# One recurrent and one convolutional projection in plain fp32 instead of a three-part split, and the convolution's taps divided anew

## The chip, the cores and the metric

The kernel runs on one core of a Trainium2 chip. Its time is device microseconds from launch to end; the time shown is the median of three runs. In the texts PE is TensorE (matrix products into PSUM), DVE is VectorE, ACT is ScalarE, POOL is GpSimd and SP is the engine whose queue issues the loads.

## The reference

A two-layer encoder works on 272 tokens (256 and 16 learned ones in front) of 1024 channels. Each layer is a token mixer and a channel mixer, each followed by `h = layer_norm(alpha * h + f(h))`. What matters here, cut down:

```
# layer 0: recurrent mixer
gate, u = split(h @ w_in)                  # w_in: 1024 x 2048
u = depthwise_conv(u, 4 taps)
r, i = sigmoid(u @ w_a), sigmoid(u @ w_x)  # eight blocks of 128, two directions
a = exp(-8 r softplus(-lam));  b = sqrt(1 - a^2) * i * u
h = scan forward + scan backward           # h_t = a_t h_(t-1) + b_t
mix = (h * gelu(gate)) @ w_out
# layer 1: convolution mixer
h = glu(x @ w_pw1 + b)                     # w_pw1: 1024 x 2048
h = depthwise_conv(h, 31 taps)
mix = silu(layer_norm(h)) @ w_pw2 + b
# both layers: expert mixer (256 wide products over u and v, the bulk of the time)
```

The output is the 256 later tokens, in fp32.

## The kernel before

Activations lie with the channels on the partitions: a tensor is eight blocks (NB) of 128 channels by 272 tokens. A projection of 1024 by 1024 is eight output blocks; the weights of each, 128 x 1024 fp32 (512 KB), come by one DMA into one of four buffers named `raw`.

Most products are made by `linears`. `load_split` makes of each weight block a rounded part `hi` in fp32r (on ACT, or on DVE where hi_on says "v") and on DVE or POOL the remainder `lo`; the activations are split the same way into `xs(k, 0)` and `xs(k, 1)`. For an output block, PE then adds up three times eight matmuls: hi by hi, hi by lo, lo by hi. With `defer=2` the first two blocks are interleaved so that the parts that are ready early go first. The buffer `raw` is free again once both parts are made.

*Recurrent mixer* (`recurrent`). x comes by four DMAs and is split block by block by `split_x`. The first eight blocks of w_in give u; `gates` takes each from PSUM (a ring of three banks), makes the four-tap convolution on DVE (L365, L369), two products per direction in plain fp32 (L376 into `pr`, L378 into `pi`, four banks), four activations on ACT, three fused operations on DVE and one on POOL. `roots` takes the square roots for four blocks at once, `scans` runs the two scans on DVE, `gelu` takes the second eight blocks of w_in (each in a bank of its own), and `gated` multiplies and splits the result into hh and hl for the output projection w_out. That goes through `linears` with `late=True`, so that its first two blocks leave the products of the last channel block to the end. `shift_in` adds the result to the residual and keeps the sums for the layer norm, whose mean is a product with a matrix of ones (L279).

*Convolution mixer* (`conformer`). `normed` centres and scales, and `norm_split` makes of it hi and lo parts (L316, L318, L324) and the fp32 value in place (L323). `conv_glu` projects through `linears` (the gating half before the other half of each block, a ring of five banks); `consume` makes the sigmoid on ACT (L1037) and the gate product hp on DVE (L1043). The 31 taps of a block are then made in one of two ways. On DVE: fused multiply-adds of 256 columns (L1071) into two sums that are added at the end (L1072). On PE: one product per tap with a diagonal matrix that ACT makes (`diagonal`, L1006). PE_TAPS says how many taps of each block PE takes; for the blocks in SPLIT the diagonals and hp are split, three fp32r products a tap, for the others it is one fp32 product. `add_up` (L763) forms the sum over blocks for the mean (L288).

What sets the order: each engine runs its instructions in a fixed order that a planner lays down before the run. It takes the instructions in program order as priority and starts each where its costs say that operands and buffers are there; `issue_after` forces an instruction behind another. An engine whose next instruction has to wait makes everything behind it wait.

Of the kernel before, what the change touches and what calls it, by code (L numbers as in the profile page):

```python
# [7 lines left out]
F32 = mybir.dt.float32  # L8
# [3 lines left out]
AF = mybir.ActivationFunctionType  # L12
OP = mybir.AluOpType
# [4 lines left out]
P = 128  # L18
D = 1024
NB = D // P  # L20
# [18 lines left out]
FULL = (("v", 1024),)  # L39
SQ_AT = 4  # L40
PE_TAPS = (0, 0, 0, 0, 12, 31, 31, 31)
SPLIT = (6, 7)
CONV_ORDER = (5, 4, 6, 7)
NEG = -3.0e38
# [15 lines left out]
class Trunk:  # L60
# [105 lines left out]
    def linears(self, srcs, xs, n, lo_on, consume, defer=0, hi_on="a", ring=(0, 1, 2), first=None, late=False):  # L166
# [7 lines left out]
        for idx, src in enumerate(srcs):  # L174
# [22 lines left out]
            else:  # L197
# [3 lines left out]
                consume(idx, ps[:, :n])  # L201

    def split_x(self, src, hi, lo, hi_on="a"):
        nc = self.nc
        if hi_on == "a":
            nc.scalar.activation(hi, src, AF.Copy)  # L206
        else:
            nc.vector.tensor_copy(hi, src)
        nc.vector.tensor_tensor(lo, src, hi.bitcast(F32), op=OP.subtract)  # L209
# [118 lines left out]
    def recurrent(self):  # L328
        tc, nc, a = self.tc, self.nc, self.a
        n = T0  # L330
        with tc.tile_pool(name="mix0", bufs=2) as sp:
            x = sp.tile([P, NB, n], F32, name="x0", bufs=1)
            xs = self.new_xs()
            self.early.append(self.load(a["w_in"][0]))
# [4 lines left out]
            self.early.append(self.load(a["w_in"][2]))  # L339
            for k in range(NB):  # L340
                self.split_x(x[:, k, :], xs(k, 0), xs(k, 1), hi_on="av"[k % 2])
            gw = sp.tile([P, 4, NB, P], F32, name="gw", bufs=1)
# [8 lines left out]
            o = _OFF["lru_b_a"]  # L351
# [69 lines left out]
            def gelu(b, ps):  # L421
# [5 lines left out]
                if b >= 4:  # L427
# [3 lines left out]
                    if b == NB - 1:  # L431
                        self.pins = [None, g.ins]
                    raw.clear()

            self.linears([a["w_in"][b] for b in range(NB)], xs, n, FULL, gates, hi_on="aaavvvvv")
            self.linears([a["w_in"][NB + b] for b in range(NB)], xs, n, FULL, gelu,
                         ring=(7, 0, 1, 2, 3, 4, 5, 6))
            for b in range(NB):
# [529 lines left out]
    def conformer(self, acc):  # L968
        tc, nc, a = self.tc, self.nc, self.a
        n, m = T0, SEQ  # L970
        with tc.tile_pool(name="mix1", bufs=2) as sp:
            x = sp.tile([P, NB, n], F32, name="x1", bufs=1)
            self.collect(sp, acc, x, n)
            self.left_pool.__exit__(None, None, None)
            xs = self.new_xs()
            self.norm_split(sp, x, n, lambda k: self.col("ln_ffn_g", k), lambda k: self.col("ln_ffn_b", k),
                            lambda k: xs(k, 0), lambda k: xs(k, 1), shifted=True)
            y = sp.tile([P, NB, m], F32, name="cy", bufs=1)
            self.conv_glu(sp, xs, y)
            x2 = x[:, :, META:]  # L980
# [43 lines left out]

    def conv_glu(self, sp, xs, y):
        tc, nc, a = self.tc, self.nc, self.a
# [6 lines left out]
        def consume(i, ps):  # L1033
# [6 lines left out]
            else:  # L1040
# [5 lines left out]
                if b in SPLIT:  # L1046
                    parts[b] = [sp.tile([P, n + HALO], F32R, tag=f"hs{i}", name=f"hs{i}", bufs=len(SPLIT)) for i in range(2)]
                    self.split_x(hp, *parts[b])

        self.linears([a["pw1"][b + o] for b in range(NB) for o in (NB, 0)], xs, n, FULL, consume, defer=2,  # L1050
                     ring=(0, 1, 2, 7, 6))
        s = META - HALO
# [4 lines left out]
        for b in range(NB):  # L1057
            taps = range(KCONV - len(on_pe[b]))
            if not taps:
                continue  # L1060
            z1 = y[:, b, :]
            z2 = sp.tile([P, m], F32, tag="odd", name="odd", bufs=2)
            for k in taps:
                z = z2 if k % 2 else z1
                w, h = self.col("conf_dw_w", k * NB + b), hps[b][:, s + k:s + k + m]
                if k == 0:
                    nc.vector.tensor_scalar(z, h, w, self.col("conf_dw_b", b), op0=OP.mult, op1=OP.add)
                elif k < taps[0] + 2:
                    nc.vector.tensor_scalar(z, h, w, None, op0=OP.mult)
                else:  # L1070
                    nc.vector.scalar_tensor_tensor(z, h, w, z, op0=OP.mult, op1=OP.add)  # L1071
            nc.vector.tensor_tensor(z1, z1, z2, op=OP.add)  # L1072
            if not on_pe[b]:
                self.add_up(sp, y, b, m)
# [116 lines left out]
```

## Time and profile before

| | us |
|---|---|
| median of three runs | 1856.66 (1856.33 to 1856.78) |
| the profiled execution | 1857.75 |
| its span, first to last instruction | 1856.0 |
| PE busy | 1793.9 (97%) |
| DVE busy | 1562.6 (84%) |
| ACT busy | 940.7 (51%) |
| POOL busy | 484.6 (26%) |

The busy time of PE counts matmuls from start to end, and neighbours overlap; the rate is read from one start to the next. The recurrent mixer fills the first 128 us, the convolution mixer lies at 905 to 1070 us; the rest is the two expert mixers.

### The profile page before, as it was taken

The numbers are of one execution on the slowest core, as the hardware profiler recorded it, in microseconds if no ns is written. First come the engines' busy times: TensorE is split into PE (matmuls) and PEld (weight loads), VectorE is DVE, ScalarE is ACT, GpSimd is POOL, SyncE is SP. The second block draws the span as 40 slices with busy tenths as digits, with TensorE's granted clock in tenths as the row PEclk, the third lists the DMA queues.
The fourth block names the chain that finished last, engine by engine and source line by source line (L and its number), as shares of the span: only waits on it lengthen the run. The fifth ranks groups of instructions, "written<-read, shape, count | busy, mean of one in ns | idle before, by whom it ended". The sixth has DMA issues, their size and how long they took to land.

```text
span 1856.0 us, 35898 instructions
## 1 busy us (share of the span) xinstructions
PE 1793.9 (97%) x13929; PEld 1714.4 (92%) x13929; DVE 1562.6 (84%) x2849; ACT 940.7 (51%) x1537; POOL 484.6 (26%) x330
## 2 busy tenths in 40 slices
PE   7899999999999999999999999999999999999997
PEld 6789998999999999999889899999999999999996
DVE  8985997889998787777699869998889987878776
ACT  5744544554444444885471545444554444445442
POOL 1112899100001232321000017993000012433310
PEclk9999999999999999999999999999999999999999
DMA  5345466855557888987541354668555568989883
GB/s 195 112 150 171 160 195 194 282 171 166 168 169 239 304 315 274 318 285 272 184 136 35 106 179 155 188 204 273 184 168 171 171 226 302 324 303 342 300 278 127
DMA packets 110235, 394.15 MB, mean 212 GB/s; under 512 B 12144, under 2 KB 13296, under 8 KB 109936
## 3 DMA queue, kind: packets, MB, share of 16 engines
q1 hardware_dynamic: 91632, 324.74, 53.6%
q0 software_dynamic: 18432, 67.12, 10.1%
q8 instruction: 109, 1.79, 0.4%
q14 instruction: 62, 0.51, 0.1%
HBM read 386.50 MB, written 5.31 MB: 211 GB/s over the span
## 4 chain that ended last, share of the span: by engine, by line
PE 81%; DVE 7%; issue 6%; POOL 3%; DMA 2%; ACT 1%; POOLq 0%; SPq 0%; DVEq 0%; ACTq 0%
PE u L172 42%; PE acc L632 20%; PE acc L636 11%; POOL lo L144 2%; PE cv L1081 2%; DVE lo L144 2%; DMA raw<-peer_v 2%; PE g L590 1%; PE g L591 1%; PE sps L522 1%; PE wide_ps L865 1%; DVE rows L900 0%; PE acc L671 0%; POOL rows L891 0%; ACT t L385 0%
## 5 line engine op out<-in xcount | busy, mean ns | idle before, releaser
L137 ACT ACTIVATE hi<-raw 128x1024 fp32r<-128x1024 f32 x587 | 620.4, 1059 | 641.1 <-PE u L172 236.2
L144 DVE TENSOR_TENSOR lo<-raw,hi 128x1024 fp32r<-128x1024 f32 x500 | 612.4, 1229 | 172.4 <-PE acc L636 63.2
L172 PE MATMUL u<-xs,hi 128*128 128x224 f32 (+3 forms) x5120 | 656.0, 279 | 15.6 <-ACT xs L206 6.4
L172 PEld LDWEIGHTS u<-xs,hi 128*128 128x128 f32 x5120 | 617.5, 191 | 20.5 <-ACT xs L318 7.2
L632 PE MATMUL acc<-w,hi 128*128 128x480 f32 (+1 forms) x1984 | 458.5, 373 | 2.0 <-DVE w L209 2.0
L632 PEld LDWEIGHTS acc<-w,hi 128*128 128x128 f32 x1984 | 354.5, 188 | 35.3 <-DVE w L209 2.3
L172 PE MATMUL u<-xs,lo 128*128 128x240 f32 (+3 forms) x2560 | 355.7, 279 | 13.6 <-POOL lo L144 10.7
L172 PEld LDWEIGHTS u<-xs,lo 128*128 128x128 f32 x2560 | 322.5, 191 | 17.5 <-POOL lo L144 12.8
L636 PEld LDWEIGHTS acc<-w,lo 128*128 128x128 f32 x2048 | 267.8, 190 | 16.9 <-DVE lo L144 6.0
L636 PE MATMUL acc<-w,lo 128*128 128x240 f32 (+1 forms) x2048 | 272.1, 274 | 3.7 <-DVE lo L144 3.6
L144 POOL TENSOR_TENSOR lo<-raw,hi 128x1024 fp32r<-128x1024 f32 x92 | 241.5, 2640 | 84.0 <-ACT hi L137 66.8
L891 POOL DMA_INDIRECT rows<-u_rows,ids x64 | 94.5, 1476 | 638.4 <-DVE sv L782 450.0
L891 POOL DMA_INDIRECT rows<-peer_v,ids x64 | 104.9, 1638 | 226.1 <-DVE few_out L926 118.6
L597 ACT ACTIVATE act_b<-g 128x368 f32<-128x368 f32 (+43 forms) x58 | 22.6, 390 | 113.4 <-DVE act_b L560 95.2
L900 DVE SCALAR_TENSOR_TENSOR rows<-rows,wide 128x1024 f32<-128x1024 f32 x64 | 78.9, 1233 | 0.6 <-DMA rows<-u_rows,ids 0.6
L926 DVE SCALAR_TENSOR_TENSOR few_out<-rows,act,few_out 128x1024 f32<-128x1024 f32 x60 | 76.7, 1278 | 0.8 <-DMA rows<-peer_v,ids 0.8
L573 DVE TENSOR_TENSOR AB<-iota,iT 128x2048 f16<-128x2048 f16 x58 | 70.4, 1217 | 0.1
L316 POOL TENSOR_SCALAR xs<-x,par 128x272 fp32r<-128x272 f32 (+1 forms) x6 | 6.0, 998 | 228.3 <-DVE x L308 165.7
L590 PE MATMUL g<-AB 128*128 128x128 f16 x464 | 58.6, 220 | 0.0
L591 PE MATMUL g<-Bl,AB 128*128 128x128 f16 x464 | 58.0, 219 | 0.0
L209 DVE TENSOR_TENSOR w<-act_b,w 128x960 fp32r<-128x960 f32 (+1 forms) x32 | 35.9, 1123 | 22.1 <-ACT w L206 21.8
L209 DVE TENSOR_TENSOR w<-act_a,w 128x960 fp32r<-128x960 f32 (+3 forms) x38 | 36.3, 969 | 18.2 <-ACT w L206 18.1
(256 smaller groups left out, 1708.6 us busy)
## 6 DMA issues: line engine op xcount, KB each, us to landing
raw<-peer_u SPq DMA_DIRECT2D x256, 512.0 KB
raw<-peer_v SPq DMA_DIRECT2D x248, 512.0 KB
raw<-w_query SPq DMA_DIRECT2D x32, 512.0 KB
raw<-pw SPq DMA_DIRECT2D x24, 512.0 KB
raw<-w_in SPq DMA_DIRECT2D x16, 512.0 KB
raw<-w_out SPq DMA_DIRECT2D x8, 512.0 KB
wide<-wide SPq DMA_DIRECT2D x8, 512.0 KB
raw<-peer_v SPq DMA_DIRECT2D x16, 256.0 KB
```

The source lines that it names most:

```text
L137: self.act_hi = nc.scalar.activation(hi, raw, AF.Copy).ins
L144: i = e.tensor_tensor(lo[:, s], raw[:, s], hi[:, s].bitcast(F32), op=OP.subtract)
L172: self.mm = nc.tensor.matmul(ps[:, :n], l[:, k, :], xs(k, r)[:, :n], start=start, stop=stop)
L209: nc.vector.tensor_tensor(lo, src, hi.bitcast(F32), op=OP.subtract)
L573: nc.vector.tensor_tensor(AB.rearrange("p x c (a b) -> p (x c) a b", b=2), keys, iT[:, c0 // HC].rearrange("p x c b -> p (x c) b")[:, :, N ...
L590: nc.tensor.matmul(ps[:, c, :], A, Bh, start=True, stop=False)
L591: nc.tensor.matmul(ps[:, c, :], A, Bl, start=False, stop=True)
L632: self.mm = nc.tensor.matmul(acc[b][:, :2 * n].rearrange("p (a t) -> p a t", a=2), hi, w[:, :, :n], start=j == 0, stop=j == NK - JG - 1, s ...
L636: self.mm = nc.tensor.matmul(main[b][:, :n], hi if p_ else lo, w[:, i, :n], start=False, stop=j == NK - 1 and not p_, skip_group_check=True)
L891: self.nc.gpsimd.indirect_dma_start(out=t, out_offset=None, in_=table, in_offset=bass.IndirectOffsetOnAxis(ap=few["ids"][:, i, k:k + 1], a ...
L900: self.nc.vector.scalar_tensor_tensor(t, t, 1.0, few["x"], op0=OP.mult, op1=OP.mult, accum_out=few["act"][:, i:i + 1])
L926: nc.vector.scalar_tensor_tensor(few["out"], t, w, few["out"], op0=OP.mult, op1=OP.add)
```

## The change

`linears_whole` multiplies the weights as they lie in `raw` with x in fp32, eight products a block in the order of k, with no split of either. It takes the place of `linears` for w_in and for w_pw1. x is no longer split in the recurrent mixer; in the convolution mixer the affine step of the layer norm is made once, in place, on ACT and POOL. Of the taps, PE gets none of block 4 (12 before), 6 of block 5 (31 before) and all of 6 and 7 as before; the rest is on DVE, but for the first two taps of each block, which ACT makes. The second sum of a block has six buffers instead of two.

```
-PE_TAPS = (0, 0, 0, 0, 12, 31, 31, 31)
+PE_TAPS = (0, 0, 0, 0, 0, 6, 31, 31)
 SPLIT = (6, 7)
-CONV_ORDER = (5, 4, 6, 7)
+CONV_ORDER = (5, 6, 7)
...
+    def linears_whole(self, srcs, x, n, consume, ring):
+        for idx, src in enumerate(srcs):
+            raw = (self.early.pop(0) if self.early else self.load(src)).rearrange("p (k n) -> p k n", k=NB)
+            ps = self.psum("u", ring)
+            for k in range(NB):
+                self.mm = self.nc.tensor.matmul(ps[:, :n], raw[:, k, :], x[:, k, :n], start=k == 0, stop=k == NB - 1)
+            consume(idx, ps[:, :n])
...
-            xs = self.new_xs()
...
-            for k in range(NB):
-                self.split_x(x[:, k, :], xs(k, 0), xs(k, 1), hi_on="av"[k % 2])
...
-            self.linears([a["w_in"][b] for b in range(NB)], xs, n, FULL, gates, hi_on="aaavvvvv")
-            self.linears([a["w_in"][NB + b] for b in range(NB)], xs, n, FULL, gelu,
-                         ring=(7, 0, 1, 2, 3, 4, 5, 6))
+            self.linears_whole([a["w_in"][b] for b in range(NB)], x, n, gates, (0, 1, 2))
+            self.linears_whole([a["w_in"][NB + b] for b in range(NB)], x, n, gelu, (7, 0, 1, 2, 3, 4, 5, 6))
...
-            xs = self.new_xs()
-            self.norm_split(sp, x, n, lambda k: self.col("ln_ffn_g", k), lambda k: self.col("ln_ffn_b", k),
-                            lambda k: xs(k, 0), lambda k: xs(k, 1), shifted=True)
+            for k in self.normed(sp, x, n, True):
+                g, b = self.col("ln_ffn_g", k), self.col("ln_ffn_b", k)
+                if k % 3 == 2:
+                    nc.gpsimd.tensor_scalar(x[:, k, :], x[:, k, :], g, b, op0=OP.mult, op1=OP.add)
+                else:
+                    nc.scalar.activation(x[:, k, :], x[:, k, :], AF.Identity, scale=g, bias=b)
+            self.pins = []
             y = sp.tile([P, NB, m], F32, name="cy", bufs=1)
-            self.conv_glu(sp, xs, y)
+            self.conv_glu(sp, x, y)
...
-        self.linears([a["pw1"][b + o] for b in range(NB) for o in (NB, 0)], xs, n, FULL, consume, defer=2,
-                     ring=(0, 1, 2, 7, 6))
+        self.linears_whole([a["pw1"][b + o] for b in range(NB) for o in (NB, 0)], x, n, consume, (0, 1, 2, 7, 6))
...
-            z2 = sp.tile([P, m], F32, tag="odd", name="odd", bufs=2)
+            z2 = sp.tile([P, m], F32, tag="odd", name="odd", bufs=6)
...
                 if k == 0:
-                    nc.vector.tensor_scalar(z, h, w, self.col("conf_dw_b", b), op0=OP.mult, op1=OP.add)
+                    nc.scalar.activation(z, h, AF.Identity, scale=w, bias=self.col("conf_dw_b", b))
                 elif k < taps[0] + 2:
-                    nc.vector.tensor_scalar(z, h, w, None, op0=OP.mult)
+                    nc.scalar.activation(z, h, AF.Copy, scale=w)
```

## Rows read from the trace of the kernel before

**Rows 1.** The page: the chain that ended last, shares of the span by engine.

```profile
PE 81%; DVE 7%; issue 6%; POOL 3%; DMA 2%; ACT 1%; POOLq 0%; SPq 0%; DVEq 0%; ACTq 0%
```

**Rows 2.** Windows: start:end length, busy by engine (instructions), PE clock, DMA share, GB/s.

```profile
5.20:97.00 91.80, 78.67 (x489) 71.40 (x490) 87.77 (x204) 62.21 (x122) 9.12 (x16) 0.94 0.44 151
97.00:121.08 24.08, 23.30 (x170) 21.93 (x168) 16.86 (x32) 10.07 (x15) 0.00 (x0) 1.00 0.48 155
934.00:943.00 9.00, 8.59 (x54) 8.37 (x55) 8.74 (x21) 5.16 (x8) 4.02 (x4) 0.81 0.00 1
943.00:984.25 41.25, 41.25 (x332) 41.25 (x332) 39.95 (x77) 35.81 (x77) 0.00 (x0) 1.00 0.61 179
984.25:1026.00 41.75, 41.75 (x278) 38.76 (x276) 41.58 (x108) 1.86 (x4) 0.00 (x0) 1.00 0.04 12
```

**Rows 3.** PE's timeline at the recurrent stage's end: start, us, what [idle before <-releaser].

```profile
92.04 0.82 PE L172 MATMUL u<-hh,hi 128*128 128x272 f32 x2 [2.35 <-ACT hh L206]
...
121.08 0.72 PE L279 MATMUL mu<-total,ones 128*128 128x272 f32 x2
```

**Rows 4.** PE's timeline in the conformer stage.

```profile
934.30 0.39 PE L172 MATMUL u<-xs,hi 128*128 128x272 f32 x1 [2.15 <-ACT xs L318]
...
984.25 18.73 PE L1081 MATMUL cv<-hp,diag 128*128 128x256 f32 x86
1002.64 22.59 PE L1081 MATMUL cv<-hs,diag 128*128 128x256 f32 x186
...
1026.25 0.70 PE L288 MATMUL mu<-total,ones 128*128 128x256 f32 x2
```

**Rows 5.** PE's timeline in the recurrent stage.

```profile
12.69 2.02 PE L172 MATMUL u<-xs,lo 128*128 128x272 f32 x8
14.51 2.09 PE L172 MATMUL u<-xs,hi 128*128 128x272 f32 x15
...
30.09 0.62 PE L376 MATMUL pr<-uc,gw 128*128 128x272 f32 x2
...
31.46 0.62 PE L378 MATMUL pi<-uc,gw 128*128 128x272 f32 x2
...
44.01 2.16 PE L172 MATMUL u<-xs,hi 128*128 128x272 f32 x16
...
47.01 1.79 PE L172 MATMUL u<-xs,hi 128*128 128x272 f32 x13
```

**Rows 6.** The tile pr: count, ns min/median/max, first and last start.

```profile
L376 PEld LDWEIGHTS pr<-uc,gw x32: 186/190/332, 19.4 to 57.6; 128*128 128x128 f32 x32
...
L381 ACT ACTIVATE thr<-pr,hb x16: 463/487/508, 20.2 to 59.8; 128x272 f32<-128x272 f32 x16
```

**Rows 7.** DVE's groups by line, 0 to 97.5 us: count, busy us, mean ns, idle before.

```profile
L144 DVE TENSOR_TENSOR lo<-raw,hi 128x1024 fp32r<-128x1024 f32 x18 | 21.9, 1222 | 0.0
...
L139 DVE CAST hi<-raw 128x1024 fp32r<-128x1024 f32 x5 | 3.6, 726 | 0.0
...
L209 DVE TENSOR_TENSOR xs<-x,xs 128x272 fp32r<-128x272 f32 x8 | 3.3, 436 | 0.1
```

**Rows 8.** DVE's timeline: the start, the step before centring, and two late taps.

```profile
5.18 0.30 DVE L208 CAST xs<-x 128x272 fp32r<-128x272 f32 x1 [3.88 <-DMA x<-h]
...
927.81 1.23 DVE L144 TENSOR_TENSOR lo<-raw,hi 128x1024 fp32r<-128x1024 f32 x1 [0.38 <-ACT hi L137]
...
1015.34 0.47 DVE L1071 SCALAR_TENSOR_TENSOR cy<-hp,par,cy 128x256 f32<-128x256 f32 x1
1015.74 0.47 DVE L1071 SCALAR_TENSOR_TENSOR odd<-hp,par,odd 128x256 f32<-128x256 f32 x1
```

**Rows 9.** DVE's groups by line, 943 to 1026 us.

```profile
L1071 DVE SCALAR_TENSOR_TENSOR cy<-hp,par,cy 128x256 f32<-128x256 f32 x69 | 32.9, 477 | 0.0
...
L144 DVE TENSOR_TENSOR lo<-raw,hi 128x1024 fp32r<-128x1024 f32 x14 | 17.1, 1218 | 0.6 <-ACT hi L137 0.6
L1043 DVE SCALAR_TENSOR_TENSOR hp<-u,par,sg 128x272 f32<-128x272 f32 x8 | 4.0, 496 | 0.9 <-ACT sg L1037 0.9
```

More of the change, by code (lines that the diff above doesn't have):

```diff
@@ L1023, in taps_early, with conv_glu @@
                     yield self.diagonal(sp, i, b, k, w)
-    def conv_glu(self, sp, xs, y):
+    def conv_glu(self, sp, x, y):
         tc, nc, a = self.tc, self.nc, self.a
```

## The prediction

> **What bounds the kernel now.** I read the page first: the chain that ended last is 81% TensorE [rows 1]. That is an average over stages, so I went on to the windows of the two stages that the change touches, and then to the timelines of TensorE (PE) and VectorE (DVE) inside them; the busy column alone misleads, because matmuls overlap, so I price them from start to start.
>
> Recurrent stage, up to the last gated block (5.2 to 97 us): DVE is busy 87.8 of 91.8 us, PE's granted clock is only 0.94, and PE holds 489 matmul records [rows 2]. At their spacing (next part) these are 425 x 0.125 + 64 x 0.2285 = 67.7 us, so PE loses 24 us here to stalls and to the half clock. The reader should see such a stall at 92.04, where the output projection waits 2.35 us for ScalarE's (ACT's) hh, and that copy waits for DVE [rows 3]. This stage is bound by DVE. After it, up to the mean at 121.08 [rows 3], PE is busy 23.3 of 24.1 us [rows 2].
>
> Conformer stage (934 to 1026 us): PE is busy in every microsecond from 943 to 1026, and DVE too (39.95 of 41.25, 41.58 of 41.75) [rows 2]. PE ends last: the convolution's final product, then ACT and one add, then the mean at 1026.25 [rows 4].
>
> **The price of the two forms.** Split: 24 matmuls of 272 columns go from 44.01 to 47.01, so 0.125 us each and 3.00 us for a block of weights [rows 5]. Unsplit fp32 is in the trace too, in the recurrent gates: line 376 has 32 records for the 16 products that line 381 reads [rows 6], so one fp32 product is two records; four products lie from 30.09 to the start of the fourth at 31.46, 0.457 us each [rows 5]. Those products change weights every time, as the new ones will. A block of 8 becomes 8 x 0.457 = 3.65 us. So the change makes PE's work longer: +0.65 us a block, +10.5 us on each stage's 16 blocks. What it gives back must come from the splits and taps.
>
> By the Trainium skill, page "TensorE: Matmul & The Clock Gate", section "Weight-path perf modes", fast weight load is off for FP32 weights. If that doubled the load against the split form's, the product would wait for its weights: two loads of about 0.38 us, 0.76 us a product, +39 us a stage. The median fp32 load in the trace is 190 ns [rows 6] and lies under a record's 228 ns, so I give this rule a chance of 0.01.
>
> **Recurrent stage, term by term.** DVE loses 16 of 18 low-part subtractions (16 x 1.22 = 19.5 us), five high-part casts (3.6) and the split of x (3.3, plus the casts) [rows 7]: about 26 us of busy time, or 25 net of the overlap between neighbours. It keeps some 62 us of work. ACT, busy 62 of 92 us now [rows 2], loses fifteen casts (11 of weights, 4 of x) and gains nothing. PE now has 128 x 0.457 + 64 x 0.2285 = 58.5 + 14.6 = 73.1 us up to its last projection, so PE becomes the bound, with some 11 us of slack on DVE.
>
> - Start: the first x lands at about 5.2 us (DVE's first split, which waits for that DMA, begins there [rows 8]), and PE can start with it; it no longer waits for split pieces. The four DMAs of x land later than the first products need them only while PE is at half clock, so I charge nothing beyond that.
> - Half clock: 8 matmuls from 12.69 to 14.51 cost 0.227 each, the next 15 take 2.09 in all, their drain included [rows 5], so even after seven microseconds of patchy work the clock was at its lower level. A first block wholly at that level costs 3.65 us more, none costs 0; I take 3.
> - Stalls: bounds 0 and the 24 us of now (half clock included). DVE and ACT have slack, three PSUM banks let PE run ahead of the gates, and the second half's eight blocks have eight banks, so PE has other work while a gate is late. I take 1.5, near the lower end.
> - Weight buffers are now held until PE has used them, not until the split: four buffers, 3.65 us each, so a load has about 11 us from issue to use. I cost it at nothing: the DMA engines' share is 0.44 in this stage [rows 2].
>
> So the last projection ends at 5.2 + 3 + 73.1 + 1.5 = 82.8. Its GELU, gating and split (some 2 us) hide behind the 42 products of the first two output blocks that need only the earlier ones. The output projection has 192 x 0.125 = 24 us, 14 square records and two for the shift (16 x 0.2285 = 3.7), and 0.7 us of gaps as now: 28.4. The mean then comes at 111.6 instead of 121.08: **9.5 us gained**.
>
> **Conformer stage, term by term.** Before it, the first block's low part no longer sits on DVE (927.81, 1.23 us) ahead of the centring [rows 8], which is on the path to PE's start at 934.30 [rows 4]. At most 1.2 us go; I take 0.8, since the mean that the centring needs comes only shortly before. The affine step now runs once, in place, on ACT and POOL; POOL's two blocks (k 2 and 5) can hold the first 8 products up: +0.4. The clock was 0.81 in the first nine microseconds [rows 2], 1.7 us lost; whether that recurs I leave half open: +0.85.
> PE then does 128 x 0.457 = 58.5, six fp32 taps instead of 43, and the 186 split taps as now. The 43 take 984.25 to 1002.64, so 0.428 each; six are 2.6; the 186 take 22.6 with the last one's drain [rows 4]. End: 933.5 + 0.4 + 0.85 + 58.5 + 2.6 + 22.6 = 1018.4, and 1.0 us from there to the mean as now: 1019.5.
> DVE: 133 fused taps (69 in the row, 64 more on the odd tile) become 168, +35 x 0.396 = +13.9 [rows 8, 9]; ten plain ones go to ACT, between -2.7 and -4.0; 14 low parts go, -17.1 [rows 9]; one more add, +0.4. Net -6 on an engine that is full from its first gated block to the end; that block needs two projections, 7.3 us after PE's start, and 0.5 for the gating [rows 9], so it is there by about 942, hardly later or earlier than now. DVE ends its part between 1019 and 1020, within a microsecond of PE. The 12 taps that go to ACT cost nothing: 14 casts and 37 diagonal tiles leave ACT, which is at 35.8 of 41.25 now [rows 2]. The scaling of the residual must now wait until PE has read x, about 993; ACT is idle then (1.9 us busy of 41.75 [rows 2]), and the sum that reads it is wanted only by the second pointwise product. The mean at 1019.5 instead of 1026.25: **6.8 us gained**.
>
> The profiled execution took 1857.75 us with its span of 1856.0; less 9.5 and 6.8 it is 1841.4. It lies 1.1 us above the median of the runs shown, 1856.66, so I forecast 1840.4. With half clock 0 to 3.65 and stalls 0 to 5 the recurrent gain is 5.5 to 14, the conformer's 5 to 8.5: the forecast's own range is 1834 to 1846.
>
> **Rivals.** Times as medians.
> - *Recurrent stage keeps half of its stalls* (12 us instead of 4.5): the gates' order on PE is fixed before the run, and a gate that waits for DVE holds up everything behind it. For it: such waits are there now; against it: DVE's slack. Gain 2 there, total 1848. Chance 0.14.
> - *DVE is the conformer's bound.* Its order is fixed too: a gated block stands among the taps, and if PE delivers it 1 us later than planned, all taps behind it wait, once for each of seven blocks: 7 us, and the gain there is gone. For it: no slack; against it: the eight waited 0.9 us in all now [rows 9]. 1847. Chance 0.10.
> - *Slower: the stalls of the recurrent stage come from the gates' own chain* (product, two tanh, exp, roots, scan), not from DVE's load. Then all 24 us stay, PE's 10.5 us come on top, and the conformer gives back 6.8: 1860. It decides as soon as more than about 21 us of PE's loss stays. Against it: DVE at 96% of the stage [rows 2]. Chance 0.08, and 0.01 for the weight loads above (about 1920).
> - *Better*: no half clock in the first block, no stalls, the DVE tail ahead of PE: 1834. Chance 0.05.
>
> **How the numbers follow.** The forecast has 0.62. A change under 0.2% (3.7 us) can't be told from none. Faster: 0.62 + 0.05, 0.10 and most of the first rival's 0.14, 0.85 in all; same 0.06, from the upper edges of the two middle rivals; slower 0.09. The range takes in the middle rivals with some spread, from 1833 to 1851, and leaves the slower ones out.
>
> **What would show it.** PE should take 3.65 us for a block of 16 records in both projections; the mean after the output projection should stand near 111.6, and the conformer's near 1019.5; PE's record spacing in the recurrent stage should have few gaps, and DVE idle time. I am wrong if PE's records there stay scattered, if the blocks take much over 3.65 us at full clock, or if DVE waits for gated blocks between taps.

## The result, and the profile after

The changed kernel takes **1840.42 us** (median of four runs, 1839.31 to 1841.13). The kernel before takes 1856.72 in the same session (1856.33 to 1859.17). The ratio is 0.9905, with a 95% interval from 0.9891 to 0.9919, so the changed kernel is about 0.95% faster. The forecast was 1840.4, its range 1833 to 1851.

| us, in the profiled execution | before | after | forecast |
|---|---|---|---|
| the execution itself | 1857.75 | 1839.31 | 1841.4 |
| span | 1856.0 | 1837.5 | |
| end of the last recurrent projection on PE | | 82.30 | 82.8 |
| recurrent stage's mean | 121.08 | 110.64 | 111.6 |
| conformer: first projection to mean | 91.95 | 86.34 | 86.0 |
| PE / DVE / ACT busy | 1793.9 / 1562.6 / 940.7 | 1789.9 / 1530.3 / 906.9 | |

The page's chain that ended last, by engine, answers to [rows 1]. PE's share rose from 81% to 84% and DVE's from 7% to 10%, while issue, POOL and DMA fell.

```profile
PE 84%; DVE 10%; POOL 2%; issue 2%; ACT 1%; DMA 1%; POOLq 0%; SPq 0%; DVEq 0%; ACTq 0%
```

The windows below (start:end length, busy by engine with instructions, PE clock, DMA share, GB/s) answer to [rows 2]. The first stands beside the first row there. DVE falls from 87.77 to 74.86 us in the same stretch, and PE, at 78.67 before, now has work in 90.76 of 91.80. That is the reversal the prediction asked for: the stage was bound by DVE and is now bound by PE. The other two are the conformer, up to the first tap on PE and from there to the last one's end.

```profile
5.20:97.00 91.80, 90.76 (x434) 75.83 (x435) 74.86 (x189) 54.90 (x112) 11.75 (x16) 1.00 0.49 171
...
924.56:983.34 58.78, 58.78 (x256) 48.66 (x257) 52.35 (x133) 19.95 (x41) 2.23 (x2) 1.00 0.42 135
983.34:1008.30 24.96, 24.96 (x200) 24.55 (x199) 24.96 (x63) 3.11 (x6) 0.00 (x0) 1.00 0.06 22
```

PE's timeline in the recurrent stage (start, us, what, [idle before <-releaser]) answers to [rows 3, 5]. Its first run of records begins with the landing of x. PE waits for DVE once in the stage, 0.95 us at 49.88, where there were 24 us of stalls and half clock. Then comes the first product of the output projection, and the mean.

```profile
5.22 8.31 PE L208 MATMUL u<-x,raw 128*128 128x272 f32 x28 [5.22 <-DMA x<-h]
13.40 0.73 PE L381 MATMUL pr<-uc,gw 128*128 128x272 f32 x2
...
49.88 0.70 PE L381 MATMUL pr<-uc,gw 128*128 128x272 f32 x2 [0.95 <-DVE uc L374]
...
82.30 2.12 PE L172 MATMUL u<-hh,hi 128*128 128x272 f32 x14
...
110.64 0.73 PE L287 MATMUL mu<-total,ones 128*128 128x272 f32 x2
```

The same view in the conformer stage answers to [rows 4]. There are 256 records in 58.78 us, 3.67 us a block, and only 12 records of fp32 taps are left of 86. PE's last tap ends near 1008.3, but the mean waits 1.69 us for DVE.

```profile
924.56 58.95 PE L208 MATMUL u<-x,raw 128*128 128x272 f32 x256 [1.75 <-ACT x L984]
983.34 2.76 PE L1088 MATMUL cv<-hp,diag 128*128 128x256 f32 x12
985.75 22.57 PE L1088 MATMUL cv<-hs,diag 128*128 128x256 f32 x186
...
1010.90 0.70 PE L296 MATMUL mu<-total,ones 128*128 128x256 f32 x2 [1.69 <-DVE total L767]
```

DVE's timeline at that place, after its last tap, answers to [rows 8]. The low part of the next projection (L144) and four sums of the residual (L271) stand between the additions that the mean needs (L1079, L1094, L767).

```profile
1006.22 0.47 DVE L1078 SCALAR_TENSOR_TENSOR cy<-hp,par,cy 128x256 f32<-128x256 f32 x1
1006.62 1.21 DVE L144 TENSOR_TENSOR lo<-raw,hi 128x1024 fp32r<-128x1024 f32 x1
1007.75 0.41 DVE L1079 TENSOR_TENSOR cy<-cy,odd 128x256 f32<-128x256 f32 x1
1008.09 0.41 DVE L271 TENSOR_TENSOR rest<-x 128x256 f32<-128x256 f32 x1
1008.43 0.41 DVE L1094 TENSOR_TENSOR cy<-cy,cv 128x256 f32<-128x256 f32 x1
...
1010.43 0.41 DVE L767 TENSOR_TENSOR total<-total,cy 128x256 f32<-128x256 f32 x1
```

DVE's groups of the stretch 924.5 to 1011 (line, engine, operation, shapes, count | busy us, mean ns | idle before) answer to [rows 9]. There are 168 fused taps instead of 133, and the gated blocks (L1051) made DVE wait once, for the first.

```profile
L1078 DVE SCALAR_TENSOR_TENSOR cy<-hp,par,cy 128x256 f32<-128x256 f32 x87 | 41.4, 481 | 0.7 <-ACT cy L1074 0.7
L1078 DVE SCALAR_TENSOR_TENSOR odd<-hp,par,odd 128x256 f32<-128x256 f32 x81 | 38.9, 481 | 0.0
L1051 DVE SCALAR_TENSOR_TENSOR hp<-u,par,sg 128x272 f32<-128x272 f32 x8 | 4.0, 499 | 5.8 <-PE u L208 5.8
```

### The profile page after: what moved, and what is told of

It is laid out like the page before. It is cut to its first block, busy times and chain, and to the rows that moved or that the text cites. A ratio compares the mean times of both kernels' runs of the same rounds, so it can differ in the third digit from the quotient of the medians.

```text
span 1837.5 us, 35134 instructions
## 1 busy us (share of the span) xinstructions
PE 1789.9 (97%) x13599; PEld 1696.7 (92%) x13599; DVE 1530.3 (83%) x2812; ACT 906.9 (49%) x1478; POOL 480.7 (26%) x328
## 3 DMA queue, kind: packets, MB, share of 16 engines
q0 software_dynamic: 18432, 67.12, 10.5%
q8 instruction: 107, 1.75, 0.4%
## 4 chain that ended last, share of the span: by engine, by line
PE 84%; DVE 10%; POOL 2%; issue 2%; ACT 1%; DMA 1%; POOLq 0%; SPq 0%; DVEq 0%; ACTq 0%
PE u L172 41%; PE acc L636 22%; PE acc L640 12%; PE u L208 3%; DVE cy L1078 2%; POOL lo L144 2%; DVE odd L1078 2%; DVE lo L144 1%; PE g L594 1%; PE g L595 1%; PE sps L526 1%; PE wide_ps L869 1%; DMA raw<-peer_v 1%; PE var L759 0%; DVE x L280 0%
## 5 line engine op out<-in xcount | busy, mean ns | idle before, releaser
L137 ACT ACTIVATE hi<-raw 128x1024 fp32r<-128x1024 f32 x560 | 592.5, 1059 | 637.2 <-PE u L172 227.2
L144 DVE TENSOR_TENSOR lo<-raw,hi 128x1024 fp32r<-128x1024 f32 x468 | 572.1, 1227 | 179.8 <-PE acc L640 65.8
L172 PE MATMUL u<-xs,hi 128*128 128x240 f32 (+3 forms) x4608 | 580.7, 278 | 3.6 <-ACT xs L326 3.5
L172 PEld LDWEIGHTS u<-xs,hi 128*128 128x128 f32 x4608 | 548.9, 191 | 5.1 <-ACT xs L326 4.5
L172 PE MATMUL u<-xs,lo 128*128 128x240 f32 (+3 forms) x2304 | 314.7, 277 | 12.7 <-POOL lo L144 11.8
L172 PEld LDWEIGHTS u<-xs,lo 128*128 128x128 f32 x2304 | 286.9, 191 | 15.0 <-POOL lo L144 13.3
L144 POOL TENSOR_TENSOR lo<-raw,hi 128x1024 fp32r<-128x1024 f32 x92 | 240.0, 2625 | 84.3 <-ACT hi L137 64.7
L208 PE MATMUL u<-x,raw 128*128 128x272 f32 x512 | 121.1, 397 | 7.0 <-DMA x<-h 5.2
L208 PEld LDWEIGHTS u<-x,raw 128*128 128x128 f32 x512 | 98.1, 192 | 28.0 <-DMA raw<-w_in 5.2
```

Of the source, the lines that this page charges most:

```text
L137: self.act_hi = nc.scalar.activation(hi, raw, AF.Copy).ins
L144: i = e.tensor_tensor(lo[:, s], raw[:, s], hi[:, s].bitcast(F32), op=OP.subtract)
L172: self.mm = nc.tensor.matmul(ps[:, :n], l[:, k, :], xs(k, r)[:, :n], start=start, stop=stop)
L208: self.mm = self.nc.tensor.matmul(ps[:, :n], raw[:, k, :], x[:, k, :n], start=k == 0, stop=k == NB - 1)
```

## The experiments

Each is a change to the changed kernel. In the kernels that compute splits for nobody, the splits' results are unused, and the expectation says so.

### The two stages apart

One kernel keeps the new recurrent projection and puts the conformer back, the other the reverse.

```diff
-PE_TAPS = (0, 0, 0, 0, 0, 6, 31, 31)
+PE_TAPS = (0, 0, 0, 0, 12, 31, 31, 31)
...
-        self.linears_whole([a["pw1"][b + o] for b in range(NB) for o in (NB, 0)], x, n, consume, (0, 1, 2, 7, 6))
+        self.linears([a["pw1"][b + o] for b in range(NB) for o in (NB, 0)], xs, n, FULL, consume, defer=2,
+                     ring=(0, 1, 2, 7, 6))
...
```

> Only the recurrent part of the change: w_in unsplit in fp32, x unsplit there; the convolution mixer as before. Theory (the two parts gain separately, each by what its own stage ends earlier): the mean after the output projection at 110.6 us as in the changed kernel instead of 121.1, the convolution mixer's stretch from TensorE's first projection to the mean at 92.0 us as before; time 1847 us. Rival (the parts depend on each other, or the expert mixers give the gain back): the mean at 110.6 but the time at 1851 or more.

```diff
...
-            self.linears_whole([a["w_in"][b] for b in range(NB)], x, n, gates, (0, 1, 2))
-            self.linears_whole([a["w_in"][NB + b] for b in range(NB)], x, n, gelu, (7, 0, 1, 2, 3, 4, 5, 6))
+            self.linears([a["w_in"][b] for b in range(NB)], xs, n, FULL, gates, hi_on="aaavvvvv")
+            self.linears([a["w_in"][NB + b] for b in range(NB)], xs, n, FULL, gelu,
+                         ring=(7, 0, 1, 2, 3, 4, 5, 6))
```

> Only the convolution mixer's part of the change: w_pw1 unsplit, taps divided anew; the recurrent mixer as before. Theory (parts gain separately): the mean of the recurrent stage at 121.1 us, the convolution mixer's stretch from the first projection to the mean at 86.3 instead of 92.0 us, 1 us less ahead of it; time 1849 us. Rival (the convolution mixer's gain needs what the recurrent part leaves behind): 1855 or more.

Measured: with the recurrent part alone 1847.35 (before in the same session 1857.81; ratio 0.9941, interval 0.9919 to 0.9963), with the recurrent mean at 110.64 and the conformer's mean 90.90 us behind its first projection. With the conformer part alone 1849.51 (0.9949, 0.9930 to 0.9969), with the recurrent mean at 120.74 and 86.32 us in the conformer. Each stage does alone what it does in the changed kernel, so stage by stage the two gains add up. The medians give 10.5 and 8.3 us, 18.8 in sum against 16.3 for the whole change; intervals this wide neither confirm nor contradict that sum. The old conformer took 90.90 us in the one and 91.95 before, with nothing changed in it. The clock goes with it: the granted clock was 1.00 in its first nine microseconds here and 0.81 there [rows 2].

### The taps back, the projection left unsplit

```diff
-PE_TAPS = (0, 0, 0, 0, 0, 6, 31, 31)
+PE_TAPS = (0, 0, 0, 0, 12, 31, 31, 31)
...
```

> The changed kernel with the taps of before on TensorE (12 of block 4, 31 of block 5), the first two taps of a block still on ScalarE, four buffers for the second sum. Theory (TensorE ends the stage at 0.428 us a tap, VectorE lies beside it): 37 taps more, 15.8 us, less the 1.7 us by which VectorE ended last: the stretch from the first projection to the mean at 100 to 101 us instead of 86.3; time 1854 to 1855 us, so that the unsplit product alone would lose what the recurrent stage gains. Rival (VectorE is the bound, TensorE has room): 35 fused taps fewer there, time 1840 or less.

Measured: 1853.36 (0.9979, 0.9966 to 0.9991), and from the first projection at 922.59 to the mean at 1023.36, 100.77 us. The unsplit projection, with the first two taps of a block on ACT, makes the conformer stage 9 to 10 us longer than the split one (91.95, or 90.90 at full clock), because PE pays 10.5 us more and is the last to end: it does not wait for DVE before this mean. The taps taken off PE are what pays for it. The reverse, the taps moved and the projection left split, was not run; DVE would then have 14 low parts and 35 more taps.

### What the recurrent gain is made of

Two kernels compute the removed splits again and throw them away: the first those of the weights, the second (run later) those of x as well.

```diff
+                hi = self.wp.tile([P, NB * P], F32R, tag="hi", name="hi", bufs=3)
+                lo = self.wp.tile([P, NB * P], F32R, tag="lo", name="lo")
+                if dead[idx] == "a":
+                    self.nc.scalar.activation(hi, raw, AF.Copy)
+                else:
+                    self.nc.vector.tensor_copy(hi, raw)
+                self.nc.vector.tensor_tensor(lo, raw, hi.bitcast(F32), op=OP.subtract)
...
```

> The changed kernel, in which the high and low parts of w_in are still made on the engines that made them before (11 casts on ScalarE, 5 on VectorE, 16 subtractions on VectorE), but nothing reads them; x stays unsplit. Theory (VectorE's load bound the recurrent stage, and taking it off is the gain): 23 us of work come back on an engine with about 11 us to spare, so the mean after the output projection comes at 120 to 124 us instead of 110.6, time 1850 to 1854 us. Rival (the gain came from the earlier start on x and from the shorter chain of a block, not from VectorE's load): the mean stays at 111 to 113, time 1841 to 1843.

Measured: 1848.03 (0.9942, 0.9922 to 0.9961), with the mean at 117.04. That is between the two expectations. DVE is full again, 40.47 of 40.50 us in the second half of the projection. The last projection ends even earlier than in the changed kernel, at 80.53, but then PE stands and waits for hh, which waits for DVE. The first fence is a window, the second is PE's timeline.

```profile
40.00:80.50 40.50, 40.50 (x177) 33.25 (x176) 40.47 (x81) 34.65 (x67) 4.14 (x8) 1.00 0.40 129
```

```profile
80.53 1.88 PE L172 MATMUL u<-hh,hi 128*128 128x272 f32 x10
84.88 0.51 PE L172 MATMUL u<-hh,hi 128*128 128x272 f32 x2 [2.48 <-ACT hh L223]
86.11 0.52 PE L172 MATMUL u<-hh,hi 128*128 128x272 f32 x2 [0.72 <-ACT hi L137]
88.22 0.82 PE L172 MATMUL u<-hh,hi 128*128 128x272 f32 x2 [1.59 <-ACT hh L223]
```

That left 4 us between 117.04 and the 121.08 of before. I had put them down to the load of x's split.

> The changed kernel, with the two-part splits of the recurrent projection's weights and of its input x computed again on the engines that had them before, the parts then read by nobody (the products stay unsplit). Theory (the whole gain of the recurrent stage is VectorE's work taken away, and the earlier start that goes with it): the recurrent mean comes where it came before the change, at 120 to 122 us, and with the conformer's 6.7 us kept the time is 1849 to 1851. Rival (the weights' splits alone matter, as when they alone were put back: mean 117.0): mean 117 to 118, time 1846 to 1847.5. If the unsplit products had a gain of their own on the path, the mean would be under 117.

Measured: 1845.27 (0.9932, 0.9912 to 0.9952), with the mean at 117.34. My theory falls and the rival's mean holds (its time, 1846 to 1847.5, is just missed): with x's split the mean comes only 0.3 us later. The other part is not load. In the split form the first output block waits for pieces of x and of the weights; in the unsplit form it waits only for x and the weights, whatever else is computed. The first use of an output block by DVE (`uc`) comes at 14.75 before and at 11.53 here, 3.2 us earlier with nearly all the load in place. Part of these 3.2 us is clock: before, PE's records were still 0.227 us apart at 14.51, and 0.125 us later [rows 5]. The first row below is of the kernel before, the second of this one.

```profile
14.75 0.57 DVE L365 TENSOR_SCALAR uc<-u,par 128x272 f32<-128x272 f32 x1 [1.62 <-PE u L172]
```

```profile
11.53 0.56 DVE L382 TENSOR_SCALAR uc<-u,par 128x272 f32<-128x272 f32 x1 [0.84 <-PE u L217]
```

So of the 10.4 us, 6.7 (117.34 to 110.64) come back with the splits' load. That the other 3.7 (121.08 to 117.34) go with the dependence taken away fits the first block but is argued, not shown: in between, PE's work and clock differ too.

Where the load costs its time can be read from the end of the last projection (the row's start) to the mean. The windows are of the kernel before, of this one (two rows) and of the changed one.

```profile
85.10:121.08 35.98, 31.20 (x211) 29.18 (x209) 28.11 (x55) 14.39 (x23) 0.00 (x0) 0.91 0.38 122
```

```profile
81.57:117.34 35.77, 31.48 (x210) 29.16 (x209) 28.93 (x58) 14.39 (x23) 0.00 (x0) 0.90 0.42 140
85.30:92.13 6.83, 4.73 (x17) 4.09 (x18) 6.83 (x16) 3.46 (x6) 0.00 (x0) 0.50 0.09 15
```

```profile
82.30:110.64 28.34, 28.27 (x210) 27.16 (x208) 17.91 (x35) 13.37 (x20) 0.00 (x0) 1.00 0.50 158
```

With the load the projection itself does not end later (81.57 against 82.30). The some 210 records of the output projection then take 7.4 us more than in the changed kernel, for two reasons. PE waits for hh, 0.60 and 2.82 us, and 0.41 us for a high part; and in the longest of these waits the granted clock falls to 0.50, its lower level, for 6.83 us. This is PE's timeline:

```profile
83.54 0.52 PE L172 MATMUL u<-hh,hi 128*128 128x272 f32 x2 [0.60 <-ACT hh L223]
86.88 0.82 PE L172 MATMUL u<-hh,hi 128*128 128x272 f32 x2 [2.82 <-ACT hh L223]
```

The kernel before has the same 6.83 us at 0.50, from 89.71 on. So a part of what looks like DVE's load is TensorE's clock, lost in the waits.

The medians don't repeat these steps one to one: this kernel's mean is 6.6 us behind the changed kernel's (110.76 in the last session), its time only 5.1 us. Between that mean and the expert mixer's first g products it takes 256.4 us, the changed kernel 260.5 and, in its second profile, 258.5. Part of that is a stretch at the lower clock right behind the mean, which one has and the other does not: from 113 to 125 us the granted clock is 0.86 in the changed kernel and, from 113 to 131, 1.00 here. In all, between mean and g, the traces record 10.2 us at a granted 0.5 in each profile of the changed kernel and none here.

### The clock ahead of the first product

Nine idle products ahead of the first projection, in the time in which PE waits for x.

```diff
+            self.idle = self.bank(5, "idle")
+            self.mm = nc.tensor.matmul(self.idle, self.ones16, self.ones16[:, None, :].to_broadcast([P, 4, P]),
+                                       start=True, stop=True)
+            self.keep_clock(8)
```

> The changed kernel with nine products of constants (128 x 512, fp16) on TensorE while it waits for the first x, so that its clock may be up when x comes. Theory (the first block ran partly at half clock, and TensorE is the bound up to the output projection): the 28 records that took 8.2 us take 6.4 to 6.9, and the mean after the output projection comes 1.3 to 1.8 us earlier than 110.6. Rival (x and the weights arrive too late for more, or the gates' chain sets the end): the first records faster, the mean within 0.5 us of 110.6.

Measured: 1839.50 (0.9907, 0.9882 to 0.9932). The time can't be told from the changed kernel's. In the trace the last projection ends at 81.03 instead of 82.30 and the mean comes at 109.39 instead of 110.64. These two windows of the same stretch, first the changed kernel, then this one, show where: 6 records against 10 in the first 2.78 us. Both rows read a granted clock of 1.00, but that is no reading: the trace's record of the clock begins only at 8.56 us in the changed kernel and at 6.39 us here, and the column counts what has no record as full. The spacing of PE's records shows the clock. It is 0.453 us at the start and 0.229 us later, and it changes at 8.5 us there and at 6.5 us here.

```profile
5.22:8.00 2.78, 2.78 (x6) 2.14 (x7) 0.89 (x2) 0.00 (x0) 0.00 (x0) 1.00 0.99 332
```

```profile
5.22:8.00 2.78, 2.78 (x10) 2.27 (x11) 1.26 (x3) 0.00 (x0) 0.00 (x0) 1.00 1.02 384
```

It tells something else, too: 1.27 us at the end of the last projection arrive as 1.25 at the stage's end. But for one wait of some 1 us for DVE, which both kernels have, PE is the bound throughout.

### POOL as the place for the splits

If DVE's load was the trouble, the split form could have been kept and its low parts given to POOL, which is nearly idle here. One kernel does that in the recurrent stage (the old split projection, all low parts but the first block's on POOL), one in the conformer (split projection on POOL, 16 taps of block 5 on PE).

```diff
...
+            self.linears([a["w_in"][b] for b in range(NB)], xs, n, lambda i: (("v" if i < 1 else "p", 1024),), gates, hi_on="aaavvvvv")
+            self.linears([a["w_in"][NB + b] for b in range(NB)], xs, n, (("p", 1024),), gelu,
+                         ring=(7, 0, 1, 2, 3, 4, 5, 6))
```

> The changed kernel with the recurrent projection split as before, but with its low parts on POOL (all but the first block's) instead of VectorE. Theory (what the change gained in this stage is the work taken off VectorE; the unsplit form itself costs TensorE 10.5 us): VectorE loses 15 x 1.22 = 18 us of 88, TensorE's work stays at 62.7 us, and the mean after the output projection comes at 103 to 108 us, earlier than the 110.6 of the change; time 1834 to 1838 us. Rival (POOL at 2.6 us a low part, with the gates' own step behind it, becomes the late one, or slows VectorE): the mean at 112 us or later.

```diff
-PE_TAPS = (0, 0, 0, 0, 0, 6, 31, 31)
+PE_TAPS = (0, 0, 0, 0, 0, 16, 31, 31)
...
+        self.linears([a["pw1"][b + o] for b in range(NB) for o in (NB, 0)], xs, n, (("p", 1024),), consume, defer=2,
+                     ring=(0, 1, 2, 7, 6), first=FULL)
```

> The changed kernel with the convolution mixer's first product split as before, but all its low parts after the first two on POOL, and 16 instead of 6 taps of block 5 on TensorE. Theory (same as for the recurrent stage): TensorE 50 + 6.9 + 22.6 us and VectorE 158 fused taps from about 9.4 us on, both end near 81 us; the stretch from the first projection to the mean is 81 to 83 us instead of 86.3, time 1835 to 1838 us. Rival (POOL's 16 low parts come late, or its work slows VectorE's taps above 0.396 us): 86 us or more.

Measured: 1867.35 (1.0055, 1.0036 to 1.0073), with the recurrent mean at 137.56; and 1870.56 (1.0068, 1.0044 to 1.0092), where the conformer's mean waits 17.75 us for DVE and comes 113.46 us behind the first projection. Both miss by some 30 us. The first fence is DVE's timeline in the second kernel, the next POOL's.

```profile
951.17 2.53 DVE L1075 SCALAR_TENSOR_TENSOR cy<-hp,par,cy 128x256 f32<-128x256 f32 x1 [2.79 <-ACT cy L1071]
953.63 0.47 DVE L1075 SCALAR_TENSOR_TENSOR odd<-hp,par,odd 128x256 f32<-128x256 f32 x1
954.02 2.67 DVE L1075 SCALAR_TENSOR_TENSOR cy<-hp,par,cy 128x256 f32<-128x256 f32 x1
956.61 0.47 DVE L1075 SCALAR_TENSOR_TENSOR odd<-hp,par,odd 128x256 f32<-128x256 f32 x1
957.01 2.65 DVE L1075 SCALAR_TENSOR_TENSOR cy<-hp,par,cy 128x256 f32<-128x256 f32 x1
```

```profile
951.00 2.41 POOL L144 TENSOR_TENSOR lo<-raw,hi 128x1024 fp32r<-128x1024 f32 x1 [0.58 <-PE u L172]
954.00 2.41 POOL L144 TENSOR_TENSOR lo<-raw,hi 128x1024 fp32r<-128x1024 f32 x1 [0.58 <-PE u L172]
956.99 2.39 POOL L144 TENSOR_TENSOR lo<-raw,hi 128x1024 fp32r<-128x1024 f32 x1 [0.59 <-PE u L172]
```

A tap that starts while POOL subtracts ends 0.3 us after POOL does, 2.5 to 2.7 us instead of 0.47. So a low part on POOL that meets a tap still takes DVE's time, about 2.1 us of it, where making it on DVE took 1.22 [rows 7]. In the recurrent kernel the groups of DVE show it as a mean: the product of t and iu takes 975 ns instead of 451 in the changed kernel. The Trainium skill, page "SBUF — State Buffer", section "SBUF: two separate sides", says that a DVE operation with two SBUF inputs and a GpSimd operation that reads SBUF exclude each other for a whole instruction. These rows agree.

The held taps are not the whole miss. In the conformer eight taps take 2.1 to 2.7 us, 16 us in all. PE also waits 6.5 us there for ACT's high parts and 4.6 for POOL's low ones, its granted clock is 0.92 from 950 to 992, and it ends its last tap 94.8 us after its start, where the expectation's terms add up to 79.5. In the recurrent stage PE waits 9.3 us for DVE's uc, 7.4 for ACT's high parts and 4.0 for POOL's low ones. How much of these waits goes back to the held operations, no run tells.

### The tail of the conformer

The mean waits for DVE, so two kernels take the foreign work out of DVE's last additions. The first gives the first low parts of the next projection to POOL, the second orders them and the four sums behind the centring (`lo_after`, `issue_after`) and has the warm start as well.

```diff
-                         FULL, out, defer=2)
+                         FULL, out, defer=2, first=(("p", 1024),))
```

> The changed kernel, in which the first two low parts of the second pointwise product's weights are made on POOL instead of VectorE. In the changed kernel one of them (1.13 us to the next start) stands on VectorE between the last tap and the last adds, and the mean waits 1.69 us for that engine. Theory (VectorE's tail, not TensorE, ends the stage now): the stretch from the first projection to the mean falls from 86.3 to 85.0 to 85.3 us, and the next product starts another 0.3 earlier; time 1.3 to 1.6 us under the changed kernel's. Rival (TensorE's last tap ends the stage): no change within 0.3 us.

Measured: 1840.91 (0.9913, 0.9885 to 0.9942), and 87.08 us from the first projection (923.76) to the mean (1010.84): longer than the 86.34 that it was to shorten. POOL made the low part at 976.46 (2.61 us), in the midst of the taps, and held one up (DVE's timeline: 2.16 us instead of 0.48). The gate product ahead of it, which reads u from PSUM, was not held:

```profile
976.77 0.49 DVE L1051 SCALAR_TENSOR_TENSOR hp<-u,par,sg 128x272 f32<-128x272 f32 x1
977.18 2.16 DVE L1078 SCALAR_TENSOR_TENSOR odd<-hp,par,odd 128x256 f32<-128x256 f32 x1
979.27 0.47 DVE L1078 SCALAR_TENSOR_TENSOR cy<-hp,par,cy 128x256 f32<-128x256 f32 x1
```

The last tap ends 1.7 us later by this, and the low part that DVE no longer makes gives back 1.1. The second low part, on POOL from 1016.02, held up a step of the norm in the same way (1.43 us instead of 0.43), so the next product began 9.74 us behind the mean instead of 9.04.

```diff
-            i = e.tensor_tensor(lo[:, s], raw[:, s], hi[:, s].bitcast(F32), op=OP.subtract)
+            with self.tc.issue_after(lo_after) if lo_after else nullcontext():
+                i = e.tensor_tensor(lo[:, s], raw[:, s], hi[:, s].bitcast(F32), op=OP.subtract)
...
+                with self.tc.issue_after(self.centered) if self.centered else nullcontext():
+                    self.sum_rest([y[:, i, :n] for i in range(3, NB)])
```

> The changed kernel with two additions: eight groups of idle products on TensorE ahead of the first projection (as in the run that warmed the clock), and the second pointwise product's first low part and the four sums of the rest issued on VectorE only after the last centring. The warm start gives 1.25 us again (recurrent mean 109.4). At the tail of the depthwise stage the last adds then wait for ScalarE's bias step behind the last tap product (1008.83 in the changed kernel's own time) and run without the others between them: the conformer's mean 0.6 us nearer to its first projection (85.7 instead of 86.3). Theory (VectorE's other work between the last adds costs the path 0.6): the time 1.3 to 1.9 below the changed kernel's in the same session. Rival (the moved work returns at once in the norm's chain of three small operations, up to 0.9 us): 0.3 to 1.3 below.

> The changed kernel itself, once more, in the same session as the others, so that a difference of one or two us is read on one chip: 1840 to 1841.5, recurrent mean 110.6, the conformer's mean 86.3 us behind its first projection.

Measured: 1838.16 (0.9897, 0.9879 to 0.9915; 1836.40 to 1840.71 in five runs) beside 1840.19 for the changed kernel again (0.9901, 0.9882 to 0.9920; 1836.54 to 1841.30). The two intervals overlap almost wholly, so this is not shown to be faster. The stage itself did more than expected: from 924.37 to the mean at 1009.16 it is 84.79 us, 1.55 less than the 86.34 of the changed kernel in both of its profiles. PE ended its taps as before, 83.8 us after its start, so this is the stage with DVE out of the way. But from the mean to the next stage's first product it is 44.00 us instead of 42.71. The scaling starts 8.24 behind the mean instead of 7.60, because three of the four sums now stand on DVE between the steps of the norm. And 16 products of the next projection take 2.57 us to the next row's start instead of 1.90. The first rows below are of this kernel, the second of the changed one.

```profile
1023.17 2.74 PE L174 MATMUL u<-cl,hi 128*128 128x256 f32 x16
1025.74 1.09 PE L174 MATMUL u<-ch,hi 128*128 128x256 f32 x8
```

```profile
1024.28 2.06 PE L172 MATMUL u<-cl,hi 128*128 128x256 f32 x16
1026.18 1.09 PE L172 MATMUL u<-ch,hi 128*128 128x256 f32 x8
```

The granted clock is 1.00 in both. In this kernel three of the 16 wait for DVE's cl: the loads of weights for them begin at 1023.93, 1024.27 and 1024.60, each 0.05 us after a cl ends, with 0.15 us idle ahead of each, and the products there stand 0.33 us apart, as the cl do, instead of 0.117. PE's weight loads show the first of these waits as a break:

```profile
1023.05 0.73 PEld L174 LDWEIGHTS u<-cl,hi 128*128 128x128 f32 x5
1023.93 1.77 PEld L174 LDWEIGHTS u<-cl,hi 128*128 128x128 f32 x11
```

The kernel before takes 2.58 us for the same 16 products (1040.28 to 1042.86). So 1.29 of the 1.55 us come back, 0.64 by the moved work, as the rival has it, and the rest by these waits. The early microsecond and a half is no longer there either when the conformer begins: its recurrent mean is 1.84 us ahead of the changed kernel's in the same session, but its first projection of the conformer starts at 924.37 against 923.57.

## Why the prediction was right, step by step

- **Price of the two forms.** Right: 3.67 us a block measured in the conformer, 3.65 forecast, at full clock. The 256 weight loads of the conformer's projection average 190 ns, as the fp32 loads of before did. The rule that fast weight load is off for FP32 weights (the Trainium skill, page "TensorE: Matmul & The Clock Gate", section "Weight-path perf modes") cost nothing here.
- **The bound changes hands in the recurrent stage.** Right, and shown three ways: by the windows, by the warm start that passes through one to one, and by the kernels with unused splits, in which PE waits at the end for hh, and ACT for DVE before it makes hh (11.2 us in all in the one with all splits). DVE's slack up to the last projection (5.20 to 82.30, where it is busy 65.39 us) was 11.7 us, where I said some 11.
- **Half clock, 3 us.** Too much: 28 records took 8.2 us instead of 6.4, so 1.8. PE had the lower level until 8.5 us, not for the whole block. In the kernel before the trace's record of the clock begins at 14.62 us, which fits the reading that it was at the lower level until then.
- **Stalls, 1.5.** 0.95. Together the two terms were 1.75 too dear. A further 1.25 us that no term had are spread over the stage, nearly all in the gates' products, so that the last projection ended at 82.30 instead of 82.8.
- **Output projection, 28.4.** 28.34. My sum has a slip here: 82.8 and 28.4 make 111.2, not the 111.6 that I wrote, so by the terms the gain was 9.9 and not 9.5. The mean came at 110.64.
- **The reason given for the gain** was too narrow. I counted DVE's load alone. 3.7 of the 10.4 us remain when all of that load is put back, with the dependence of the first products on the split pieces gone; and of the load's 6.7 a part is the clock that falls in PE's waits. The sum did not suffer, because it was built from PE's side: the start at the landing of x was a term of its own.
- **Before the conformer, 0.8.** 0.24. DVE's centring now waits 0.96 us for ACT instead of standing behind the low part; from the expert mixer's mean to the first projection it is 6.61 us instead of 6.85.
- **POOL's blocks and half clock in the conformer, 1.25.** Not paid: the granted clock was 1.00 and the 256 records ran on at their price.
- **PE's end and DVE's tail.** PE ended 83.7 us after its start, where 84.9 were forecast. DVE ended its part at 86.3, within the forecast 85.5 to 86.5 (1019 to 1020 less the start at 933.5). The mean at 86.34 against 86.0 is near, but by two errors that nearly cancel: PE was 1.2 us early, and from its last tap to the mean it is 2.6 us where I took 1.0. It is DVE that ends last, which I had put level with PE. What stands in the tail was there before as well (a low part at 1021.95, among the last additions); only then PE was later.
- **Twelve taps on ACT at nothing, the scaling of the residual too.** Right. DVE waited 0.67 us once for ACT's first tap, ACT was busy 23.5 us in the stage.
- **The sum.** The means moved by 10.4 and the conformer's stretch by 5.6 (4.6 against the recurrent-only kernel's 90.90, whose clock was not disturbed), where 9.5 and 6.0 stood. A further 1.3 us lie behind the conformer's mean (42.71 instead of 44.03), which I had no term for: the first product of the second projection comes 0.65 us sooner after the mean, and 16 of its products take 1.90 us instead of 2.58. From the recurrent mean to the conformer's first product 0.7 us are lost. At the end of the second stage the profiled execution is 16.7 us ahead (1053.61 against 1070.28 for the same product); the rest up to 18.5 comes in the second layer's expert mixer, where nothing was changed. The medians differ by 16.3, as forecast, but with terms off by up to 1.7 each, a mixer that gives or takes two and the slip of 0.4, agreement to a tenth of a microsecond is luck.

Of the rivals, none came true as it was told. DVE did not wait for gated blocks after the first; the gates' chain did not hold PE; the weight loads did not double. Of the second rival one half did: DVE ends the conformer, by 1.7 us and by its tail, not by 7 us of waits among the taps.

What stays open is why the early gains drift between the recurrent mean and the conformer, where nothing was changed. The thirteen profiles have 809.9 to 815.8 us for it. A part goes with the clock: the two with no time at a granted 0.5 there take 809.9 and 811.9 us, the six with 10.2 us of it take 812.8 to 815.8. Up to 3 us are left at equal clock, and no run separated cause from chance.

## What to carry to other kernels

A split costs on the engine that makes the parts, and it makes the first products wait for the parts. So where the splitting engine is the bound, a product of 22% more PE time can still win. Where PE is the bound it lost: the conformer's projection alone cost 9 us until taps were moved with it. A wait of PE can cost more than its length, since the clock may fall in it. Before moving work to an idle neighbour, look in the trace for operations of the busy engine that will run beside it, since idle is not the same as independent. Forecast from the engine that will be the bound, as a sum of start, work and stalls, and put the other engine's end beside it: where the two ends lie within a microsecond, what the planner has put into the tail decides.

## What the runs showed of the hardware that I had not expected

- A DVE operation with two inputs from SBUF takes 2.1 to 2.7 us instead of 0.47 when a subtraction on POOL (2.41 us) is under way. One with an input in PSUM took its 0.49 us beside such a subtraction. POOL is held as well: beside DVE's taps one of its subtractions took 5.63 us.
- In the first 2.78 us of work PE's records stood 0.453 us apart, twice their later spacing. The column of the granted clock read 1.00 there only because its record begins later, at 8.56 us; with idle products ahead it begins at 6.39, and 10 records fit into the same time instead of 6.
- In the kernel with all splits put back, PE waited 0.60 and 2.82 us for hh, and in the second wait the granted clock fell to 0.50 for 6.83 us. In the changed kernel, which does not wait there, it is 1.00 throughout.
